# A fourth step in the stick-breaking pipeline, and four moves around it, in a two-layer decoder kernel

## The chip, the cores and the metric

The kernel is one program on one core of a Trainium2 chip. The metric is the device time of one execution in microseconds (us); the time of the kernel before is the median of three executions. One further execution was recorded by the hardware profiler, and every duration below is from that one.

## The reference

One inference step of a decoder with two layers, for a prompt of 1024 tokens and for 8 samples of one token each, which share all weights. The width is 1024, every attention has 4 heads of 128, the feed-forward width is 2816, and the memory has 256 tokens. Cut to what the change touches:

```python
# layer 0 (mixer A): gated linear recurrence beside attention into the memory
o, S = hgrn2_scan(q, k, v, logf, s0)            # a 128x128 state per head; s0 given for the samples
o = rmsnorm(o, hg_gain) * silu(g_h)             # the "gate"
om = mem_attend(q_m, mem_k, mem_v)              # softmax over 256 memory tokens
out = concatenate([o, om]) @ w_o
# layer 1 (mixer B): stick-breaking attention beside attention into the memory
z = einsum('bqhd,bkhd->bhqk', q, kf) * scale + bf
log_keep = where(mask, log_sigmoid(-z), 0.0)
tail = cumsum(log_keep, reverse) - log_keep     # for each query, over its keys
w = where(mask, exp(log_sigmoid(z) + tail), 0.0); o = einsum('bhqk,bkhd->bqhd', w, vf)
# both layers
h = h + rmsnorm(mix, g[1])
h = h + rmsnorm(swiglu(rmsnorm(h, g[2]), w_gu, w_down), g[3])
```

Outputs are the two streams, the recurrence states, the shared keys and values, and the memory's keys and values. All is in 32-bit floats.

## The kernel before

**Tiles.** The 1024 prompt tokens are two groups, 0 and 1, of G = 512; the 8 samples ride with group 1, which so has 520 columns. Activations lie with features on the 128 partitions and tokens along the row. TensorE works in a reduced-precision float, so each operand is split in a high part (a copy on ScalarE) and a low part (a subtraction on VectorE), and a product is three matmuls: high by high, high by low, low by high. Weights are split as they arrive (`split_w`, L207: a load, the copy of L217, the subtraction of L218). `proj` (L223) is such a product over 8 blocks; its matmuls are those of L231. The feed-forward block of some parts uses a seven-product scheme instead (`gate_up_w`, L619).

**Order.** The program is written as generators that yield after each step. `weave` (L187) takes streams with a declared number of steps and always advances the one whose share done, steps taken by declared steps, is least; a stream that has more steps than declared takes the rest when the others have ended. Each engine has one queue, and its order is fixed before the run by a planner: of the instructions that by its own reckoning of durations are ready, an engine gets the one that comes first in the woven program. So an instruction whose inputs are late in the plan is passed by later ones, but on the chip a queue keeps the order it was given. `tc.issue_after(x)` ties an instruction behind x on x's engine.

**Buffers.** `C()` is a pool of 4 tiles of 128x1024, `B()` of 7 tiles of 128x512, `A()` of 8 tiles of 128x1040, and `S()` of 3 banks of PSUM.

**Stick-breaking (`sb_prompt`, L1583).** Per head there are 3 units of work in group 0 and 7 in group 1. A unit is: scores on TensorE (L1594), offset and mask on VectorE (L1605 to L1609), two activations on ScalarE (`softplus`, L1580 and L1581), a running sum (L1614) and a subtraction (L1616) on VectorE, an exponential on ScalarE (L1617). The weights so made are transposed on TensorE one unit later (`turn`, L1623) and multiplied with the values two units later (`values`, L1634); `step` (L1645) holds this order. The intermediate `e` is a `B()`.

**Memory attention (`mem_attn`, L1008)** has the same shape: scores (L1032), softmax, `turn` (L1019), values (L1051), and `put` writes a head's result to the operand `xo`. For layer 0 and group 1 it runs after the gates' `merge`, beside the samples' own memory attention (`ms`) and the rest of the feed-forward block of group 0 (L1843).

**The samples' recurrence (`hgrn_sample`, L1298)** runs a head at a time: two loads of 128x1024 (the states, and the values broadcast to all partitions), three products and one sum on VectorE (L1332, L1335, L1336, L1341), a store of the states, and sums over the partitions by matmul (`total`, L1318). At the end the result goes to DRAM and back to change its layout (L1351, L1353), is transposed (L1358) and normed (L1365). It is woven beside the gate and part 1 of the feed-forward block (L1833).

**Residual (`residual`, L419)** loads the stream kept in DRAM in four pieces, all issued ahead of its loop (L428).

**The end (`close`, L807, and `out_rows`, L885).** The last down projection is made for 264 columns (three row blocks) and then for 256 (two). For each of 8 row blocks m of features: product (L823), sum (L828), square (L830), scale (L833). After m = 7 the first half of the features is transposed to rows and copied (`turn(0)`, L897, L902); `finish` sums the squares by matmul (L912), takes the root (L920, L921), and for each block of 128 tokens transposes the second half, does two fused multiply-adds (L926, L929) and stores 128x1024 (L934).

## Time and profile before

| what | value |
|---|---|
| median of three executions | 2404.62 us (2404.5 to 2404.99) |
| the profiled execution's own time | 2406.1 us |
| its span, first to last instruction | 2404.4 us |
| TensorE busy | 2377.7 us, 99% |
| VectorE busy | 1710.3 us, 71% |
| ScalarE busy | 1322.5 us, 55% |
| moved by DMA | 357.60 MB, mean 149 GB/s |

The profiled execution took 1.7 us more than its span and 1.5 us more than the median. In the rows, PE is TensorE's matmuls and PEld its weight loads, DVE is VectorE, ACT ScalarE, POOL GpSimd and SP SyncE; SPq is SyncE issuing a DMA. A row of a timeline gives start, duration, engine, line, operation, output and inputs, shapes, the number of instructions merged, and in brackets how long the engine had been idle and what ended that.

### The profile page before, as it was taken

The page shows a single profiled execution, that of the slowest core. Times are in us where ns is not written, and L with a number is a line of the kernel's source. Part 1 is how long each engine was busy: PE and PEld are TensorE (multiplying, and loading weights), DVE is VectorE, ACT ScalarE, POOL GpSimd, SP SyncE. Part 2 cuts the span into 40 slices and gives each one's busy share as a digit, 9 for nine tenths or more (in the row PEclk, how much of TensorE's full clock was granted, in tenths as well). Part 3 has the DMA queues.
Part 4 walks back from the last instruction along what each step waited for, and adds up shares of the span by engine and source line. Part 5 has one row for each costly group of instructions (what it writes and reads, how often), then busy time and mean ns, then how long its engine had stood idle before and what let it go on. Part 6 is the DMA issues. An engine that isn't in the chain of part 4 may idle for free.

```text
span 2404.4 us, 42487 instructions
## 1 busy us (share of the span) xinstructions
PE 2377.7 (99%) x15962; PEld 2156.4 (90%) x15962; DVE 1710.3 (71%) x3195; ACT 1322.5 (55%) x2736; POOL 113.7 (5%) x187
## 2 busy tenths in 40 slices
PE   9999999999999999999999999999999999999998
PEld 7888989888889988999999989877778989999998
DVE  5867558766776676878556677777776679676866
ACT  5547544454664554667544554568457566554445
POOL 1001202100000000000001200111000000000000
PEclk9999999999999999999999999999999999999999
DMA  6454766677535447332659746545354354343342
GB/s 198 122 165 119 174 199 161 164 197 193 168 106 166 134 154 232 94 101 88 193 168 225 205 152 194 161 137 156 108 154 125 95 158 137 106 129 100 113 125 76
DMA packets 514641, 357.60 MB, mean 149 GB/s; under 512 B 20173, under 2 KB 463674, under 8 KB 514434
## 3 DMA queue, kind: packets, MB, share of 16 engines
q1 hardware_dynamic: 498562, 312.93, 43.8%
q0 software_dynamic: 15872, 41.95, 7.4%
q8 instruction: 126, 2.06, 0.4%
q14 instruction: 81, 0.66, 0.1%
HBM read 322.86 MB, written 65.49 MB: 162 GB/s over the span
## 4 chain that ended last, share of the span: by engine, by line
PE 85%; DVE 6%; ACT 4%; DMA 3%; issue 2%; SPq 0%; DVEq 0%; ACTq 0%
PE mm L231 37%; PE q L619 18%; PE q L791 11%; PE q L545 4%; PE mm L1235 2%; PE s L1414 1%; DMA b<-qd 1%; PE s L1051 1%; PE s L1032 1%; PE mm L968 1%; PE mm L995 1%; PE q L823 1%; DVE ws L218 1%; ACT c L1123 1%; DVE b L1614 1%
## 5 line engine op out<-in xcount | busy, mean ns | idle before, releaser
L231 PE MATMUL mm<-x,ws 128*128 128x512 f32 (+1 forms) x5016 | 924.4, 342 | 2.2 <-ACT a L1470 1.1
L231 PEld LDWEIGHTS mm<-x,ws 128*128 128x128 f32 x5016 | 774.8, 188 | 111.4 <-ACT a L1470 1.3
L217 ACT CAST ws<-w 128x512 fp32r<-128x512 f32 x596 | 346.6, 584 | 396.1 <-PE mm L231 228.4
L218 DVE TENSOR_TENSOR ws<-w,ws 128x512 fp32r<-128x512 f32 x596 | 381.1, 646 | 238.5 <-ACT ws L217 230.5
L791 PE MATMUL q<-m,ws 128*128 128x260 f32 (+1 forms) x2496 | 303.9, 283 | 0.1
L791 PEld LDWEIGHTS q<-m,ws 128*128 128x128 f32 x2496 | 299.9, 188 | 1.0 <-ACT m L238 0.3
L619 PE MATMUL q<-y,ws 128*128 128x260 f32 (+1 forms) x1920 | 249.3, 284 | 1.9 <-DVE t L654 1.7
L619 PEld LDWEIGHTS q<-y,ws 128*128 128x128 f32 x1920 | 237.6, 188 | 3.2 <-DVE t L654 1.9
L619 PE MATMUL q<-x,ws 128*128 128x260 f32 (+1 forms) x1668 | 219.7, 283 | 1.3 <-DVE ws L614 0.7
L619 PEld LDWEIGHTS q<-x,ws 128*128 128x128 f32 x1668 | 207.7, 188 | 2.2 <-DVE ws L614 1.1
L231 PE MATMUL mm<-m,ws 128*128 128x512 f32 x768 | 186.1, 396 | 0.0
L612 ACT CAST ws<-w 128x512 fp32r<-128x512 f32 x206 | 125.0, 619 | 96.8 <-PE q L791 30.8
L231 PEld LDWEIGHTS mm<-m,ws 128*128 128x128 f32 x768 | 142.9, 188 | 32.0
L614 DVE TENSOR_TENSOR ws<-w,ws 128x512 fp32r<-128x512 f32 x206 | 139.4, 688 | 44.9 <-ACT ws L612 41.6
L800 DVE TENSOR_TENSOR r<-r,q 128x260 f32<-128x260 f32 (+1 forms) x160 | 60.6, 420 | 46.8 <-PE q L791 46.5
L545 PE MATMUL q<-x,ws 128*128 128x260 f32 (+1 forms) x720 | 87.0, 282 | 0.0
L545 PEld LDWEIGHTS q<-x,ws 128*128 128x128 f32 x720 | 86.3, 188 | 0.2
L238 ACT CAST m<-t 128x512 fp32r<-128x512 f32 (+1 forms) x88 | 54.7, 622 | 37.5 <-DVE t L860 19.8
L612 ACT CAST ws<-b 128x512 fp32r<-128x512 f32 x82 | 50.6, 620 | 42.5 <-PE q L791 13.4
L614 DVE TENSOR_TENSOR ws<-b,ws 128x512 fp32r<-128x512 f32 x82 | 56.5, 689 | 20.6 <-ACT ws L612 19.9
L239 DVE TENSOR_TENSOR m<-t,m 128x512 fp32r<-128x512 f32 (+1 forms) x88 | 60.9, 691 | 13.5 <-ACT m L238 12.5
L290 DVE TENSOR_TENSOR st<-st,n 128x512 f32<-128x512 f32 (+1 forms) x91 | 62.3, 692 | 3.7 <-ACT n L289 2.2
(422 smaller groups left out, 3117.0 us busy)
## 6 DMA issues: line engine op xcount, KB each, us to landing
w<-in_w_gu SPq DMA_DIRECT2D x275, 256.0 KB
w<-in_w_down SPq DMA_DIRECT2D x160, 256.0 KB
wsum<-in_w_gu POOLq DMA_DIRECT2D x48, 512.0 KB, 6.1
w<-in_w_in_a SPq DMA_DIRECT2D x80, 256.0 KB
w<-in_w_o SPq DMA_DIRECT2D x64, 256.0 KB
w<-wsum SPq DMA_DIRECT2D x61, 256.0 KB
b<-in_w_gu SPq DMA_DIRECT2D x39, 256.0 KB
b<-wsum SPq DMA_DIRECT2D x39, 256.0 KB
```

What stands on the lines that cost most here:

```text
L217: nc.scalar.copy(ws[:, 0, :n, :], raw[:, :n, :])
L218: split[0] = nc.vector.tensor_sub(ws[:, 1, :n, :], raw[:, :n, :], ws[:, 0, :n, :].bitcast(F32))
L231: nc.tensor.matmul(ps[:, a, : PW[g]], wt, xt[k][:, xi, o : o + PW[g]], start=(k == 0 and wi == 0), stop=(k == nk - 1 and wi == 2),)
L238: nc.scalar.copy(dst[0], src)
L239: nc.vector.tensor_sub(dst[1], src, dst[0].bitcast(F32))
L290: nc.vector.tensor_add(acc[:, :n], acc[:, :n], t[:, :n])
L545: ins = nc.tensor.matmul(pp[a][:, :h], wt, xt[k][:, xi, a * h : (a + 1) * h], start=(k == 0 and wi == 0), stop=(k == ND - 1 and wi == 2),)
L612: nc.scalar.copy(w[:, 0, :], src)
L614: split[0] = nc.vector.tensor_sub(w[:, 1, :], src, w[:, 0, :].bitcast(F32))
L619: nc.tensor.matmul(ps[:, :h], w[:, wj, k * P : (k + 1) * P], x[:, xi, :], start=(first and k == 0 and wi == 0), stop=(k == 3 and wi == 2), ...
L791: nc.tensor.matmul(pp[a][:, :h], wt, mids[k][:, xi, a * h : (a + 1) * h], start=(k == 0 and wi == 0), stop=(k == nf - 1 and wi == 2),)
L800: nc.vector.tensor_add(d, d, pp[a][:, :h])
```

## The change

Seven edits, all in the text below:

- `sb_prompt`: `step` keeps one more unit between the scores and `turn`, so that weights are transposed two units after their scores and used three units after; three closing steps instead of two; `e` is half of a `C()` tile, two units sharing one. The streams that hold it declare one step more.
- `residual`: the first two pieces are loaded ahead of the loop, the third at k = 0, the fourth at k = 2, where the stream comes from DRAM.
- `close` and `out_rows`: the first half of the features is transposed after m = 5; the scaling of m = 7 moves from ScalarE to VectorE and into a tile of its own; the transposes of the second half go feature block by feature block over all row blocks; the closing sums and the stores go by halves of 512 features.
- `mem_attn` takes a function for its result. For layer 0, group 1, it runs beside the recurrence, the gate and part 1, and its result is parked in the recurrence's key tiles (`parked`); `unpark` splits it into `xo` where the attention stood before.
- `hgrn_sample` goes by four samples (half a head): eight rounds with one `C()` each in place of four with two.
- `mixer_b.load`: the split of what is loaded is tied behind the last weight split.
- `a1.open()` stands after the weave of the recurrence.

```diff
@@ -420,13 +420,19 @@
         ht = [xpool.tile([P, 2, w], F32, tag=f"x{g}", name=nm("ht")) for _ in range(ND // 2)]
-        for j in range(ND // 2):
+
+        def fetch(j):
             if first:
 ...
                 nc.sync.dma_start(ht[j], hs[g][:, 2 * j : 2 * j + 2, :n])
+
+        for j in range(ND // 2 if first else 2):
+            fetch(j)
         for k in range(ND):
+            if not first and k % 2 == 0 and k < 4:
+                fetch(k // 2 + 2)
             if first:
@@ -830,9 +836,13 @@
                         nc.vector.tensor_add(acc, acc, sq)
-                    nc.scalar.activation(R, R, AF.Copy, scale=gcol(l, 3, m))
-                    if m == 7:
-                        list(rows.turn(0))
+                    if m < ND - 1:
+                        nc.scalar.activation(R, R, AF.Copy, scale=gcol(l, 3, m))
+                    else:
+                        rows.last = T()[:, :h]
+                        nc.vector.tensor_scalar(rows.last, R, gcol(l, 3, m), None, op0=ALU.mult)
+                    if m == 5:
+                        rows.first()
                     if m % 2:
@@ -890,18 +900,24 @@

-        def turn(self, i):
+        def first(self):
             for c, n in self.rows:
 ...
                 for k in range(4):
-                    nc.tensor.transpose(
-                        ps[:n, k * P : (k + 1) * P], self.R[4 * i + k][:, c * P : c * P + n], ident
-                    )
-                if i == 0:
-                    self.yt[c] = xpool.tile([P, D], F32, tag="x0", name=nm("yT"))
-                    nc.scalar.copy(self.yt[c][:n, :512], ps[:n, :])
-                else:
-                    yield c, n, ps
+                    nc.tensor.transpose(ps[:n, k * P : (k + 1) * P], self.R[k][:, c * P : c * P + n], ident)
+                self.yt[c] = xpool.tile([P, D], F32, tag="x0", name=nm("yT"))
+                nc.scalar.copy(self.yt[c][:n, :512], ps[:n, :])
+
+        def second(self):
+            pts = [S() for _ in self.rows]
+            for k in range(4):
+                for (c, n), ps in zip(self.rows, pts):
+                    src = self.R[4 + k][:, c * P : c * P + n]
+                    if k == 3:
+                        o = (c - 2 * self.a) * P
+                        src = self.last[:, o : o + n]
+                    nc.tensor.transpose(ps[:n, k * P : (k + 1) * P], src, ident)
+            return pts

@@ -921,19 +937,18 @@
                     rr[c0 + c] = r[:n, c : c + 1]
-            for c, n, pt in self.turn(1):
-                yt, h, rc = self.yt[c], (ht[c] if c < CH else hsm), rr[c]
-                nc.vector.scalar_tensor_tensor(
-                    yt[:n, :512], yt[:n, :512], rc, h[:n, :512], op0=ALU.mult, op1=ALU.add
-                )
-                nc.vector.scalar_tensor_tensor(
-                    yt[:n, 512:], pt[:n, :], rc, h[:n, 512:], op0=ALU.mult, op1=ALU.add
-                )
-                if c < CH:
-                    t0 = G + c * P
-                    nc.sync.dma_start(y_prompt[0, t0 : t0 + P, :], yt)
-                else:
-                    nc.sync.dma_start(y_sample.rearrange("b o d -> (b o) d"), yt[:NB])
+            pts = self.second()
+            for i in range(2):
+                s = slice(512 * i, 512 * i + 512)
+                for (c, n), pt in zip(self.rows, pts):
+                    yt, h = self.yt[c], (ht[c] if c < CH else hsm)
+                    src = pt[:n, :] if i else yt[:n, s]
+                    nc.vector.scalar_tensor_tensor(yt[:n, s], src, rr[c], h[:n, s], op0=ALU.mult, op1=ALU.add)
+                    if c < CH:
+                        t0 = G + c * P
+                        nc.sync.dma_start(y_prompt[0, t0 : t0 + P, s], yt[:, s])
+                    else:
+                        nc.sync.dma_start(y_sample.rearrange("b o d -> (b o) d")[:, s], yt[:NB, s])
                 yield
@@ -1005,7 +1020,7 @@

-    def mem_attn(g, l, qm, xo):
+    def mem_attn(g, l, qm, out):
         mkt, mv = C(), C()
@@ -1034,7 +1049,7 @@
             if pr:
-                put(xo, H + h, slice(0, G), po)
+                out(h, po)

@@ -1299,14 +1314,16 @@

-        def fetch(h):
-            st, vb = C(), C()
-            for t, src in (
-                (st, state_hgrn[0, :, h].rearrange("b k v -> k b v")),
-                (vb, vd[:, h * P : (h + 1) * P].partition_broadcast(P)),
+        def fetch(i):
+            h, a = divmod(i, 2)
+            t = C()
+            bs = slice(4 * a, 4 * a + 4)
+            for d, src in (
+                (t[:, 0], state_hgrn[0, bs, h].rearrange("b k v -> k b v")),
+                (t[:, 1], vd[bs, h * P : (h + 1) * P].partition_broadcast(P)),
             ):
-                nc.sync.dma_start(t.rearrange("p a (b v) -> p (a b) v", v=P), src)
-            return st, vb
+                nc.sync.dma_start(d.rearrange("p (b v) -> p b v", v=P), src)
+            return t

@@ -1321,28 +1338,27 @@

-        for h in range(H):
+        for h, a in ((h, a) for h in range(H) for a in range(2)):
             def col(t):
-                return t[h // 2][:, h % 2, G : G + NB].unsqueeze(2).to_broadcast([P, NB, P])
-
-            st, vb = nxt
-            nxt = h < H - 1 and fetch(h + 1)
-            stv, vbv = (t.rearrange("p a (b v) -> p (a b) v", v=P) for t in (st, vb))
+                o = G + 4 * a
+                return t[h // 2][:, h % 2, o : o + 4].unsqueeze(2).to_broadcast([P, 4, P])
+
+            st, vb = nxt[:, 0], nxt[:, 1]
+            nxt = 2 * h + a < 2 * H - 1 and fetch(2 * h + a + 1)
+            stv, vbv = (t.rearrange("p (b v) -> p b v", v=P) for t in (st, vb))
             with tc.issue_after(split[0].ins):
                 nc.vector.tensor_mul(stv, stv, col(Ft))
-            yield
             with tc.issue_after(split[0].ins):
 ...
             nc.vector.tensor_add(st, st, vb)
-            nc.sync.dma_start(st_sample[0, :, h].rearrange("b k v -> k b v"), stv)
+            nc.sync.dma_start(st_sample[0, 4 * a : 4 * a + 4, h].rearrange("b k v -> k b v"), stv)
             total()
 ...
                 nc.vector.tensor_mul(vbv, stv, col(Qt))
-            for a in range(2):
-                qs = B(F32R), B(F32R)
-                split_to(qs, vb[:, a, :])
-                late.extend((h, a, i, p) for i, p in enumerate(qs))
+            qs = B(F32R), B(F32R)
+            split_to(qs, vb)
+            late.extend((h, a, i, p) for i, p in enumerate(qs))
             yield
@@ -1517,7 +1533,18 @@
         def mem(self):
-            yield from mem_attn(self.g, 0, self.Qm, self.xo)
+            yield from mem_attn(self.g, 0, self.Qm, lambda h, po: put(self.xo, H + h, slice(0, G), po))
+
+        def parked(self, h):
+            return self.K[h // 2][:, h % 2, :G]
+
+        def mem_parked(self):
+            yield from mem_attn(self.g, 0, self.Qm, lambda h, po: nc.scalar.copy(self.parked(h), po))
+
+        def unpark(self):
+            for h in range(H):
+                put(self.xo, H + h, slice(0, G), self.parked(h))
+                yield

@@ -1607,7 +1634,10 @@
                 nc.vector.tensor_scalar(zb[:, i:o], ps[:, i:o], bh, 44.0, op0=ALU.add, op1=ALU.min)
-            e = B()
+            if not spare:
+                c = C()
+                spare.extend((c[:, 0], c[:, 1]))
+            e = spare.pop(0)
             softplus(zb, e, o)
@@ -1640,12 +1670,12 @@

-        po, asked, turned = [None, None], None, None
+        po, asked, scored, turned, spare = [None, None], None, None, None, []

         def step(new=None):
-            nonlocal asked, turned
+            nonlocal asked, scored, turned
             old, turned = turned, asked and (*asked[0], *turn(*asked[1]))
-            asked = new
+            asked, scored = scored, new
             if old:
@@ -1657,7 +1687,7 @@
                 yield
-        for _ in range(2):
+        for _ in range(3):
             step()
@@ -1700,7 +1730,8 @@
                 x = X(self.g)
-                split_to((x[:, 0, :n], x[:, 1, :n]), t)
+                with tc.issue_after(split[0].ins):
+                    split_to((x[:, 0, :n], x[:, 1, :n]), t)
                 self.xo.append(x)
@@ -1708,7 +1739,7 @@
         def mem(self):
-            yield from mem_attn(self.g, 1, self.Qm, self.xo)
+            yield from mem_attn(self.g, 1, self.Qm, lambda h, po: put(self.xo, H + h, slice(0, G), po))

@@ -1829,8 +1860,8 @@
     weave((a1.core(), 22), (f0.part(0), 14), (islice(ms, 9), 9), (islice(w0, 16), 17))
+    weave((a1.sample(), 16), (a1.gate(), 4), (a1.mem_parked(), 11), (f0.part(1), 14), (w0, 9))
     a1.open()
-    weave((a1.sample(), 16), (a1.gate(), 4), (f0.part(1), 14), (w0, 9))

@@ -1840,7 +1871,7 @@

-    weave((chain(a1.merge(), a1.mem()), 36), (ms, 74), (rest(), 33))
+    weave((chain(a1.merge(), a1.unpark()), 20), (ms, 74), (rest(), 33))
     xk0, xb0 = [], []
@@ -1854,7 +1885,7 @@
     fw = ffn_w(1, 0, o1.x, (5, 6, 5), 0, False, beside=(0, 1), src=o1.R)
-    weave((chain(b0.sb(), b0.mem()), 25), (chain(fw.part(0), fw.part(1)), 28))
+    weave((chain(b0.sb(), b0.mem()), 26), (chain(fw.part(0), fw.part(1)), 28))
     p4 = fw.part(4)
@@ -1876,7 +1907,7 @@
     weave(
-        (chain(b1.sb(), b1.mem()), 40), (chain(b1.sb_sample(), b1.mem_sample()), 76),
+        (chain(b1.sb(), b1.mem()), 41), (chain(b1.sb_sample(), b1.mem_sample()), 76),
         (chain(f0.part(0), f0.part(1), f0.part(2), islice(p3, 8)), 48),
```

## The prediction

> **What bounds the kernel now.** I read the page first, then the waits of TensorE, then the stages that the change touches.
>
> ```profile
> PE 2377.7 (99%) x15962; PEld 2156.4 (90%) x15962; DVE 1710.3 (71%) x3195; ACT 1322.5 (55%) x2736; POOL 113.7 (5%) x187
> ```
>
> TensorE is busy for 2377.7 of 2404.4 us. The change takes no matmul away. So no more than 26.7 us of idle TensorE can be won, whatever the other engines gain; the question is whose waits these are. Its waits, with total, count and longest:
>
> ```profile
> PE s L1623 <- ACT b L1617: 6.8, 8, 1.7
> ...
> PE mm L231 <- ACT a L1470: 1.1, 1, 1.1
> ...
> PE mm L231 <- DVE ws L218: 1.0, 1, 1.0
> ...
> PE s L1019 <- DVE b L1068: 0.5, 1, 0.5
> ```
>
> The largest entry is the transposing of stick-breaking weights that ScalarE has not finished: 6.8 us in 8 waits. By stage (start and end, length, then busy time of PE, PEld, DVE, ACT, POOL, clock, DMA share, GB/s), in this order the recurrence of the samples, the memory attention after it, and the two stick-breaking stages:
>
> ```profile
> 498.00:616.00 118.00, 118.00 (x606) 98.23 (x606) 80.44 (x115) 53.52 (x97) 9.41 (x16) 1.00 0.76 205
> 616.00:702.00 86.00, 85.50 (x392) 68.62 (x391) 67.53 (x131) 63.31 (x164) 0.00 (x0) 1.00 0.44 132
> 972.00:1094.00 122.00, 120.95 (x948) 115.22 (x948) 94.89 (x193) 76.91 (x165) 0.00 (x0) 1.00 0.34 102
> 1519.00:1886.00 367.00, 361.12 (x1729) 288.16 (x1728) 264.37 (x421) 225.17 (x503) 26.72 (x24) 1.00 0.45 137
> ```
>
> The stick-breaking stages leave TensorE idle for 1.05 and 5.88 us, which is the 6.8 again. The recurrence's stage leaves it nothing idle, the memory attention's 0.5 us. So one edit of the seven aims at a real wait; the others can win little and can lose.
>
> **The change part by part.** *The fourth step.* One unit, from the waits and the order of time:
>
> ```profile
> 1772.17 1.02 PE L1594 MATMUL s<-a,a 128*128 128x512 f32 x2
> ...
> 1775.94 0.62 DVE L1605 TENSOR_SCALAR b<-s,biasp 128x384 f32<-128x384 f32 x1
> ...
> 1779.48 1.02 PE L1594 MATMUL s<-a,a 128*128 128x512 f32 x2
> ...
> 1781.56 0.63 ACT L1617 ACTIVATE b<-b 128x512 f32<-128x512 f32 x1 [1.97 <-DVE b L1616]
> ...
> 1782.24 0.66 PE L1623 MATMUL s<-ident,b 128*128 128x128 f32 x4 [1.74 <-ACT b L1617]
> ```
>
> Scores at 1772.17, finished weights at 1782.19: 10.0 us, of which 2.8 pass between the end of the scores and VectorE's coming to them, behind weight splits. The next unit's scores are at 1779.48, 7.3 us later, and TensorE's queue has the transposes right behind those; it waits 1.74 us for them, and the feed-forward block's products behind them wait too. With one more unit between, the transposes stand behind the scores after that, about 7 us further on, while the longest of the 8 waits is 1.7. I take the whole 6.8 as gone. At least nothing is won, if the late engine is only waited for elsewhere; at most 12.8, the idle time of the weight loads at the same line:
>
> ```profile
> PEld s L1623 <- ACT b L1617: 12.8, 12, 2.6
> ```
>
> What it costs: the one extra closing step holds no instruction of its own. `e` in half a `C()` leaves the samples' loads two or three of four tiles in the stage at 1519. There 32 loads share 367 us, 11.5 us each; with two tiles one may live 22.9 us. From issue to use a load takes some 5.4 us (the chain below), its scaling or multiplying and the next step perhaps 10 more, an estimate, so it stays hidden. What is late next: VectorE is busy for 264 of 367 us and ScalarE for 225, so neither becomes the bound.
>
> ```profile
> 1649.99 5.41 DMA c<-in_cache_sb_v,pidx
> ```
>
> *The closing.* Rows of the end, after the last sum L828:
>
> ```profile
> 2394.92 1.04 PE L897 MATMUL s<-ident,r 128*128 128x128 f32 x8
> ...
> 2395.12 0.42 DVE L828 TENSOR_TENSOR r<-r,q 128x256 f32<-128x256 f32 x1
> 2395.55 0.58 ACT L902 COPY yT<-s 128x512 f32<-128x512 f32 x1 [0.46 <-PE s L897]
> ...
> 2396.04 0.42 ACT L830 ACTIVATE n<-r 128x256 f32<-128x256 f32 x1
> ...
> 2397.81 0.75 DVE L926 SCALAR_TENSOR_TENSOR yT<-yT,rr,hT 128x512 f32<-128x512 f32 x1 [2.27 <-ACT rr L921]
> ...
> 2400.57 0.33 SPq L934 DMA_DIRECT2D out_y_prompt<-yT  x1
> ```
>
> From the end of L828 (2395.54) to the first multiply-add (2397.81) pass 2.27 us, in which ScalarE also does two copies (the first is shown, 0.58) and the scale. With these gone from that place the square starts at once, 0.5 us earlier (2395.54 for 2396.04), and the root, which had the second copy and the scale ahead of it, I put 0.2 earlier still: 0.7 won. But the first eight transposes, 1.04 us, ran beside that wait; after m = 5 they stand on TensorE's path and push L828 back by about 0.9. The sum is +0.2. The multiply-adds stay four; the last store is issued at the same distance from the first of them, but carries 256 KB in place of 512. From its issue at 2400.57 to the end at 2404.4 pass 3.8 us. The half that goes would take 1.3 us at 205 GB/s, the rate of the stage at 498, and nothing if latency sets the end; I take 0.7, the middle. Together -0.5, between -1.1 and +0.2. For the 264 columns nothing changes: TensorE has the 256 columns' products behind them.
>
> *The residual's loads.* In the stage of the heads of layer 1, group 1, weights wait behind them:
>
> ```profile
> 1471.63 1.39 SPq L428 DMA_DIRECT2D ht<-hs  x3
> ...
> 1473.62 8.45 DMA w<-in_w_in_b
> ...
> 1489.35 2.67 PE L231 MATMUL mm<-x,ws 128*128 128x260 f32 x20 [1.01 <-DVE ws L218]
> ```
>
> TensorE waits twice afterwards, here and once for L1470: 2.1 us together, both in the waits above. But three of the four pieces still go in the first step (two ahead, the third at k = 0), so one of four leaves the burst; the waits stand 7 us after the weights landed (1482.07), behind VectorE's order. I take a quarter, -0.5, between -2.1 and +1: the fourth piece may now come late for L442, which VectorE's weight splits stand behind. The split tied in `load` adds no instruction; what hides it are the products of the block's last part, 0:
>
> ```profile
> 1308.73 40.09 PE q L619 x324
> ```
>
> *The memory attention moved.* It was not limiting where it stood (0.5 us idle); that wait, L1019 above, goes: -0.5. In the new place TensorE is never idle, so its products only lengthen the stage and shorten the next. Two costs come with it. The recurrence's `total` holds one of three `S()` banks throughout, so scores, transposes and results of the attention share two; a transpose may have to wait for a bank. The nearest row is the same L1019 wait with three banks, 0.5 once in eight; I take +0.5, between 0 and 4 (0.5 in all eight). Parking adds four copies on ScalarE of some 0.6 us, `unpark` four splits that `put` did before; ScalarE is busy for 53.5 of 118 us there, so 0. The gate's tiles come free later, as the keys stay; they now follow the memory queries, which end in that stage: 0.
>
> POOL, 9.4 us busy in that stage, makes weight sums on marks of products that don't move, and SyncE only gets the two loads of keys and values in the stage before: 0.
>
> *The recurrence by halves.* One of its four lines, its loads, and copy and subtraction of 128x512:
>
> ```profile
> L1332 DVE TENSOR_TENSOR c<-c,a x4: 1219/1219/1221, 503.7 to 559.4; 128x1024 f32<-128x1024 f32 x4
> L1308 SPq DMA_DIRECT2D c<-in_state_hgrn x4: 368/368/822, 448.9 to 536.5; - x4
> L612 ACT CAST ws<-w 128x512 fp32r<-128x512 f32 x206 | 125.0, 619 | 96.8 <-PE q L791 30.8
> ...
> L614 DVE TENSOR_TENSOR ws<-w,ws 128x512 fp32r<-128x512 f32 x206 | 139.4, 688 | 44.9 <-ACT ws L612 41.6
> ```
>
> VectorE's 16 instructions of 128x1024 at 1.22 become 32 of 128x512 at 0.69: 19.5 to 22.1 us, +2.6 of an engine with 37.6 to spare: 0. The SP queue gets 12 DMAs more (8 loads, 4 stores) at 0.37 each, 4.4 us in 118. The first load leads its use by 55 us and the last by 23; half a head ahead in place of a whole one leaves some 11, an estimate, still above a leg of 3.3 (below): 0. The place that matters is the end: the generator has 20 steps now (1 + 16 + 3), but its stream still declares 16. So the last four steps are taken when the gate, part 1 and the attention have ended:
>
> ```profile
> 598.08 1.08 PE L1318 MATMUL s<-b,selr 128*8 128x512 f32 x4
> ...
> 599.55 0.67 DVE L1349 COPY b<-s 8x512 f32<-8x512 f32 x1
> 600.25 0.30 SPq L1351 DMA_DIRECT2D od<-b  x1
> ...
> 603.57 0.31 SPq L1353 DMA_DIRECT2D b<-od  x1
> ...
> 613.00 0.41 PE L1358 MATMUL s<-ident,b 8*128 8x8 f32 x4
> ...
> 616.19 0.64 DVE L1365 SCALAR_TENSOR_TENSOR a<-ss,par,ss 128x8 f32<-128x8 f32 x4
> ```
>
> Before, TensorE had part 1 between 603 and 613. Now the chain is: last product, copy and subtraction 0.69 + 0.62 + 0.69, two matmuls 0.5, copy 0.67, two legs through DRAM at 3.3 each (600.25 to 603.57 is one), transposes to L1365 3.8: 13.6 us. Its cover is part 2 of the feed-forward block, which needs none of it and of which TensorE has eight products like this one, from the chain; the planner may bring them forward, since it passes what isn't ready:
>
> ```profile
> 652.12 5.55 PE mm L231 x24
> ```
>
> Uncovered it costs 13.6; covered, only what the plan errs on a leg by. I take +1.5, half a leg, between 0 and 13.6.
>
> Sum: -6.8 - 0.5 - 0.5 - 0.5 + 0.5 + 1.5 = -6.3 us. The profiled execution took 2406.1, 1.5 above the median of 2404.62; on the median the forecast is 2398.3.
>
> **The rivals.** *The waits move on.* Removed waits of 0.2 to 1.7 us come back where TensorE next needs VectorE: in the same stage its weights are split by an engine that is 72% busy in a fixed order. For it: the 2.8 us between scores and L1605 is VectorE's lateness, which the step doesn't cure. Against it: in that stage no wait on L218 is among TensorE's largest, and five tiles of split weights lie between. If half of the 6.8 comes back, 2401.7; if all, 2405.1: no change.
>
> *The bare end of the recurrence* (the other side). If the plan puts L1358 ahead of part 2's products, because it reckons the legs short, TensorE stands still for them. It decides when more than 12.6 of the 13.6 us are bare: 2398.3 - 1.5 + 13.6 = 2410.4, and an idle TensorE may start slowly. At the start of the kernel, after such an idle time, the first 12 products took 3.78 us and later ones 2.75:
>
> ```profile
> 7.67 3.78 PE mm L1235 x12
> ...
> 11.89 2.75 PE mm L1235 x12
> ```
>
> That adds 1.0: 2411.4. Against it: no wait of TensorE on a DMA appears past the start of the kernel in the waits. [...]
>
> *The small transfers.* [...] As a mechanism here: the stage at 498 already moves 205 GB/s at a DMA share of 0.76, and it gets 12 DMAs more, with only half a head loaded ahead. If each made VectorE's queue, and through it the weight splits, late by the 1.0 us that a late broadcast row cost it (below), 12 us come on: 2410.3. Against it: the lead of some 11 us, and that TensorE has no idle time there.
>
> ```profile
> 607.91 1.23 DVE L1098 TENSOR_TENSOR c<-c,b 128x1024 f32<-128x1024 f32 x1 [1.01 <-DMA b<-qd]
> ```
>
> **How the numbers follow.** 0.2%, 4.8 us, is about what a measurement of this kernel can tell from no change: faster is below 2399.8, slower above 2409.4. The forecast has 0.57; its own range, with the small terms at their ends, is 2392 to 2401, so a little of it counts as no change, as does nearly all of the first rival, 0.26. The bare end has 0.10, the small transfers 0.05, and 0.02 is left for orders of the plan that I don't foresee. Faster 0.58 (with the first rival's lucky part), same 0.27, slower 0.15. The range leaves out the worst of the slower cases and the best of the upper bounds: 2391 to 2409.
>
> **What would show it.** The fourth step: no L1623 among TensorE's waits, and the stage at 1519 shorter by some 6 us at the same work. The closing: L897 in two groups, one ahead of the products of m = 6; the first multiply-add about 1.7 us after the last L828; the last store's issue to the end about 3.1 us. The residual: L428 in groups of three and one. The recurrence's end: L1358 surrounded by products of part 2 and without a wait of over 2 us; a wait there of 5 us or more makes the prediction wrong, as does a stage of stick-breaking in which L231 waits for L218 as long as L1623 did.

## The result, and the profile after

The changed kernel takes 2413.88 us (median of 8 runs, 2410.02 to 2416.25), the kernel before beside it on the same chip 2405.68 us (8 runs, 2404.5 to 2408.9). The ratio is 1.0028 with a 95% interval of 1.0018 to 1.0038: slower. The profiled execution took 2412.47 us with a span of 2410.7; that of before had 2406.1 and 2404.4. So 6.3 us more of span are to be explained where I had forecast 6.3 us less. The medians differ by 8.2 us; what the single traces can't place of that is said where the terms are summed.

Line numbers below L420 are the same in both kernels; further down they have moved: the recurrence's first multiplication is L1350 now, the attention's transposes L1034, the scores L1621, `softplus` L1607 and L1608, the transposes of stick-breaking weights L1653, the group-0 feed-forward products L625. The first line of the page, of the changed kernel:

```profile
PE 2381.8 (99%) x15962; PEld 2159.9 (90%) x15962; DVE 1713.1 (71%) x3213; ACT 1324.4 (55%) x2738; POOL 112.4 (5%) x187
```

The number of matmuls is the same, 15962, but TensorE is busy for 4.1 us longer. Part of the loss is therefore no wait in the profile's sense: products that were stretched. The granted clock is at half for 3.41 us once in the middle of the changed kernel (below), and at the start its first record at full begins at 12.93 us where it did at 9.73. If half of such a time is lost, these are 1.7 and 1.6 us, estimates, 3.3 of the 4.1. TensorE's waits, of the changed kernel (total, count, longest):

```profile
PE mm L231 <- DVE ws L218: 3.3, 2, 2.4
...
PE s L1034 <- ACT b L1077: 2.8, 1, 2.8
PE q L625 <- DVE ws L620: 2.3, 4, 1.1
...
PE q L625 <- ACT ws L618: 1.5, 2, 1.3
...
PE mm L231 <- ACT b L1647: 1.2, 1, 1.2
```

The transposes of stick-breaking weights (L1623 before, 6.8 us in 8 waits) are gone from the list, as the change intends. In their place stand four others that the kernel before did not have at this size: 2.4 us once for weights of the projections (L218), 2.8 us once for the exponentials of the memory attention (L1077), and 3.8 us for split weights of the feed-forward blocks (L618 and L620), 3.0 of them beside group 0's stick-breaking. Of the last the kernel before has this much (L612 and L614 there):

```profile
PE q L619 <- DVE ws L614: 1.0, 3, 0.6
...
PE q L619 <- ACT ws L612: 0.2, 1, 0.2
```

By stage (same columns as in the prediction), of the changed kernel: recurrence with memory attention, the rest of that stage, and the two stick-breaking stages:

```profile
498.00:650.00 152.00, 148.84 (x749) 123.30 (x749) 96.07 (x172) 72.20 (x150) 8.96 (x16) 0.99 0.63 173
650.00:712.00 62.00, 61.01 (x270) 47.39 (x269) 54.49 (x91) 47.59 (x119) 0.00 (x0) 1.00 0.51 157
980.00:1107.00 127.00, 122.37 (x953) 116.08 (x952) 95.86 (x196) 78.61 (x167) 0.00 (x0) 1.00 0.38 115
1527.00:1893.00 366.00, 364.83 (x1770) 293.63 (x1768) 265.53 (x424) 227.72 (x505) 30.33 (x28) 1.00 0.47 143
```

TensorE's idle time fell from 5.88 to 1.17 us in the stage of group 1, the last row; it rose from 1.05 to 4.63 us in the stage of group 0, the third, and from 0.5 to 4.15 us in the first two, where the clock column shows 0.99 in place of 1.00.

To compare stretches of equal work I cut the trace of each kernel by TensorE's own work: each matmul counts with the median distance from its start to the next start, by its shape and line in the kernel before, and the cuts lie where the same sum is reached. This is worked out from the starts of all 15962 matmuls; in the kernel before the cuts fall at 512.2, 724.5, 985.5, 1197.1, 1503.4 and 1935.2 us. The times between them, in us:

| kernel | start | recurrence, memory attention | to group 0 | stick-breaking, group 0 | to group 1 | stick-breaking, group 1 | to the end | span |
|---|---|---|---|---|---|---|---|---|
| before | 512.2 | 212.4 | 261.0 | 211.6 | 306.3 | 431.8 | 469.2 | 2404.4 |
| after | 514.3 | 218.6 | 260.8 | 216.3 | 305.8 | 426.1 | 468.8 | 2410.7 |
| difference | +2.1 | +6.2 | -0.2 | +4.7 | -0.5 | -5.7 | -0.4 | +6.3 |

The start holds none of the edits but the move's first loads and lies between 512.2 and 514.5 in all profiled kernels of this study, so 2 us of a single execution hang on it. Between the two kernels of the table TensorE's waits for the first rows (L399) differ by 0.7 us (1.9 and 2.6), and the later rise of the clock accounts for 1.6, the estimate above. So the change does win 5.7 us where it was meant to, and loses 6.2 and 4.7 in two other places. Those two places are what the experiments had to explain.

### The profile page after: what moved, and what is told of

It is laid out like the page before. It is cut to its first block, busy times and chain, and to the rows that moved or that the text cites. A ratio compares the mean times of both kernels' runs of the same rounds, so it can differ in the third digit from the quotient of the medians.

```text
span 2410.7 us, 42477 instructions
## 1 busy us (share of the span) xinstructions
PE 2381.8 (99%) x15962; PEld 2159.9 (90%) x15962; DVE 1713.1 (71%) x3213; ACT 1324.4 (55%) x2738; POOL 112.4 (5%) x187
## 4 chain that ended last, share of the span: by engine, by line
PE 91%; DVE 4%; ACT 2%; DMA 1%; issue 1%; SPq 0%; ACTq 0%; DVEq 0%
PE mm L231 41%; PE q L625 18%; PE q L797 12%; PE q L551 4%; PE mm L1250 2%; PE s L1430 1%; PE s L1664 1%; PE s L1047 1%; PE s L1066 1%; PE s L1621 1%; PE mm L983 1%; PE mm L1010 1%; PE q L829 1%; PE s L551 1%; PE s L1034 1%
## 5 line engine op out<-in xcount | busy, mean ns | idle before, releaser
L231 PE MATMUL mm<-x,ws 128*128 128x512 f32 (+1 forms) x5016 | 929.6, 342 | 5.7 <-DVE ws L218 3.3
L231 PEld LDWEIGHTS mm<-x,ws 128*128 128x128 f32 x5016 | 776.5, 189 | 117.1 <-DVE ws L218 4.3
L218 DVE TENSOR_TENSOR ws<-w,ws 128x512 fp32r<-128x512 f32 x596 | 380.5, 645 | 222.5 <-ACT ws L217 217.9
L625 PE MATMUL q<-y,ws 128*128 128x260 f32 (+1 forms) x1920 | 250.4, 284 | 0.6 <-ACT q L633 0.4
L625 PEld LDWEIGHTS q<-y,ws 128*128 128x128 f32 x1920 | 238.0, 188 | 2.9 <-DVE ws L620 0.8
L625 PE MATMUL q<-x,ws 128*128 128x260 f32 (+1 forms) x1668 | 220.0, 283 | 3.9 <-DVE ws L620 2.1
L625 PEld LDWEIGHTS q<-x,ws 128*128 128x128 f32 x1668 | 207.8, 188 | 4.9 <-DVE ws L620 2.7
L231 PE MATMUL mm<-m,ws 128*128 128x512 f32 x768 | 186.7, 397 | 0.0
L618 ACT CAST ws<-w 128x512 fp32r<-128x512 f32 x206 | 124.9, 619 | 97.2 <-PE q L797 30.7
L231 PEld LDWEIGHTS mm<-m,ws 128*128 128x128 f32 x768 | 142.5, 188 | 32.1 <-DVE ws L218 0.2
L620 DVE TENSOR_TENSOR ws<-w,ws 128x512 fp32r<-128x512 f32 x206 | 139.3, 688 | 43.4 <-ACT ws L618 40.3
L618 ACT CAST ws<-b 128x512 fp32r<-128x512 f32 x82 | 50.6, 620 | 42.7 <-PE q L797 13.4
L239 DVE TENSOR_TENSOR m<-t,m 128x512 fp32r<-128x512 f32 (+1 forms) x88 | 60.9, 691 | 15.4 <-ACT m L238 14.5
L620 DVE TENSOR_TENSOR ws<-b,ws 128x512 fp32r<-128x512 f32 x82 | 56.4, 688 | 21.4 <-ACT ws L618 21.1
```

The source lines that it names most:

```text
L218: split[0] = nc.vector.tensor_sub(ws[:, 1, :n, :], raw[:, :n, :], ws[:, 0, :n, :].bitcast(F32))
L231: nc.tensor.matmul(ps[:, a, : PW[g]], wt, xt[k][:, xi, o : o + PW[g]], start=(k == 0 and wi == 0), stop=(k == nk - 1 and wi == 2),)
L239: nc.vector.tensor_sub(dst[1], src, dst[0].bitcast(F32))
L618: nc.scalar.copy(w[:, 0, :], src)
L620: split[0] = nc.vector.tensor_sub(w[:, 1, :], src, w[:, 0, :].bitcast(F32))
L625: nc.tensor.matmul(ps[:, :h], w[:, wj, k * P : (k + 1) * P], x[:, xi, :], start=(first and k == 0 and wi == 0), stop=(k == 3 and wi == 2), ...
```

## What stood in the two places

The chain in the recurrence's stage, of the changed kernel, in order of time:

```profile
561.22 0.69 DVE L239 TENSOR_TENSOR b<-c,b 128x512 fp32r<-128x512 f32 x1 [0.18 <-ACT b L238]
561.93 0.37 SPq L1325 DMA_DIRECT2D c<-in_state_hgrn  x1
...
567.49 0.69 DVE L1350 TENSOR_TENSOR c<-c,a 128x512 f32<-128x512 f32 x1 [3.82 <-DMA c<-in_state_hgrn]
...
569.29 0.68 DVE L1071 TENSOR_REDUCE nmx<-s 128x2 f32<-128x512 f32 x1
...
570.67 0.46 ACT L1077 ACTIVATE b<-s,nmx 128x256 f32<-128x256 f32 x1
...
571.73 0.66 PE L1034 MATMUL s<-ident,b 128*128 128x128 f32 x4 [2.80 <-ACT b L1077]
```

The load of the fifth half head (L1325) is issued at 561.93, right when the last reader of the third (L239) lets go of its tile at 561.91: the attention holds two of the four `C()` tiles for its keys and values, so the halves take turns in the other two. VectorE comes to the multiplication L1350 at 567.49 less 3.82, that is at 563.67: 1.7 us after the load was issued, while the load takes 5.6. VectorE stands still for 3.82 us, and behind L1350 in its queue stands the maximum for the memory attention (L1071), behind that ScalarE's exponentials, and behind these TensorE. Then, of the same kernel, the stretch of the wait and the one behind it:

```profile
569.00:571.70 2.70, 0.00 (x0) 0.00 (x0) 2.70 (x5) 2.64 (x8) 0.00 (x0) 1.00 0.07 22
571.70:575.00 3.30, 3.27 (x19) 3.27 (x20) 1.61 (x6) 2.17 (x4) 0.00 (x0) 0.65 0.30 86
```

After 2.8 us of idle TensorE the granted clock falls: 0.65 in the mean of 3.3 us. In the trace it is 0.5 from 572.71 on, for 3.41 us. If half of that time is lost again, it is 1.7 us, an estimate, and the profile calls TensorE busy meanwhile (3.38 us of the 3.38 from 572.72 to 576.10).

The stage of group 0, of the changed kernel:

```profile
1021.02 1.02 PE L1621 MATMUL s<-a,a 128*128 128x512 f32 x2
...
1022.32 1.03 PE L1621 MATMUL s<-a,a 128*128 128x128 f32 x4
...
1024.57 0.63 ACT L1608 ACTIVATE c<-c 128x512 f32<-128x512 f32 x1
1024.62 0.60 PE L1621 MATMUL s<-a,a 128*128 128x256 f32 x2
...
1025.75 0.63 ACT L1608 ACTIVATE c<-c 128x512 f32<-128x512 f32 x1
1026.29 0.60 ACT L618 CAST ws<-c 128x512 fp32r<-128x512 f32 x1
...
1026.94 0.51 PE L625 MATMUL q<-x,ws 128*128 128x260 f32 x2 [1.28 <-ACT ws L618]
...
1028.55 1.47 PE L625 MATMUL q<-x,ws 128*128 128x260 f32 x10 [1.10 <-DVE ws L620]
```

Scores are issued three times within 3.6 us, ScalarE does their softplus together, and the split of the weight that TensorE needs next (L618) comes behind. That weight (`c<-in_w_gu`) is late too: its load is issued at 1022.46 and has landed, by its semaphore, at 1026.23, 0.06 us before the split. Whether this order came from the fourth step or from `e` in half a `C()` tile the two traces can't say; both were changed at once.

## The experiments

Theory A: the three groups of the change act separately, and the loss is in the move with the halves and in group 0's fourth step. Rival B: `e` in `C()` tiles costs in both groups, or the small edits (loads, closing, split) shift the plan. The first runs separate the groups.

**The fourth step alone**, both groups, with `e` in `C()`; the rest as before.

```diff
-            e = B()
+            if not spare:
+                c = C()
+                spare.extend((c[:, 0], c[:, 1]))
+            e = spare.pop(0)
...
-            asked = new
+            asked, scored = scored, new
...
-        for _ in range(2):
+        for _ in range(3):
```

> The kernel before with the fourth step alone (and e in half a C tile), in both groups. Theory A: the step wins some 5.7 us in the stage of group 1 and loses some 4.8 in that of group 0, where TensorE waits for weight splits instead, so the whole stands 1 us below the kernel before. Rival: the loss in group 0 comes from the other edits' changed order and not from the step; then the whole is 6 us below.

2406.2 us (2404.26 to 2407.7) beside 2404.68 for the kernel before, ratio 1.0006 [0.9997, 1.0016]. Group 1's stretch takes 426.9 us (431.8 before), group 0's 216.8 (211.6). So the fourth step alone wins 4.9 us and loses 5.2, near the 5.7 and 4.8 of theory A: it is worth nothing as a whole that can be measured, and the two halves of it have opposite signs.

**The move of the memory attention and the halves alone.**

```diff
-    weave((a1.sample(), 16), (a1.gate(), 4), (f0.part(1), 14), (w0, 9))
+    weave((a1.sample(), 16), (a1.gate(), 4), (a1.mem_parked(), 11), (f0.part(1), 14), (w0, 9))
+    a1.open()
...
-    weave((chain(a1.merge(), a1.mem()), 36), (ms, 74), (rest(), 33))
+    weave((chain(a1.merge(), a1.unpark()), 20), (ms, 74), (rest(), 33))
```

> The kernel before with the memory attention moved beside the recurrence and the recurrence by halves, nothing else. Theory A: this pair is the largest loss, 6 to 7 us above the kernel before, with a wait of about 2.8 us of the memory attention's transposes (for the exponential, which stands behind a product of the recurrence whose states land late) and about 2 us of later waits for weight splits. Rival: these waits are an accident of the whole change's order; then it stands within 2 us of the kernel before.

2411.8 us (2409.87 to 2414.47), ratio 1.003 [1.0017, 1.0042]. The recurrence's stretch takes 218.7 us, as after the whole change (218.6). TensorE's and VectorE's waits of this kernel, one row each:

```profile
PE s L1019 <- ACT b L1062: 2.8, 1, 2.8
```

```profile
DVE c L1335 <- DMA c<-in_state_hgrn: 3.8, 1, 3.8
```

They are the same two waits as after the whole change (there L1034 and L1350), with the same half clock behind them (at 571.8; the mean clock of this execution is 0.997, and 0.999 in the kernel before). This group carries most of the slowdown: 7.1 us by the medians, where theory A had 6 to 7.

**The rest alone**: residual loads, closing by halves, the tied split.

```diff
-        for j in range(ND // 2):
+        for j in range(ND // 2 if first else 2):
...
-                    if m == 7:
-                        list(rows.turn(0))
+                    if m == 5:
+                        rows.first()
...
-                split_to((x[:, 0, :n], x[:, 1, :n]), t)
+                with tc.issue_after(split[0].ins):
+                    split_to((x[:, 0, :n], x[:, 1, :n]), t)
```

> The kernel before with the spread residual loads, the closing by halves and the tied split of the load alone. Theory A: next to nothing, 0 to 2 us below the kernel before (0.2 at the end, and up to 2 us that may go at the last products of the block of layer 1, group 0). Rival: the spread loads cost the 1.4 us that the heads of layer 1, group 1, wait longer in the changed kernel; then it stands 1 to 2 us above.

2406.22 us, ratio 1.0005 [0.9996, 1.0015]: no change that can be measured. No stretch moves by more than 0.8 us, but for the start (513.5) and the one up to group 1 (304.1 for 306.3), where the kernel before has a wait of 1.7 us at 1349 that comes and goes between kernels with the same code there: with the fourth step in group 1 only, the stretch takes 304.0, in the next run, which differs only behind it, 306.1. The total lies where the rival put it, but the longer wait of the rival isn't there: that for L218 is 0.8 us (1.0 before). The medians of these three runs lie 1.5, 7.1 and 1.5 us above the kernel before; their sum, 10.2, agrees with the 8.2 of the whole change within the intervals, as it should if the groups act separately.

**The fourth step in group 1 only.** Group 0 keeps three steps, two closing ones, and `e` in `B()`.

```diff
-            if not spare:
+            if g and not spare:
...
-            e = spare.pop(0)
+            e = spare.pop(0) if g else B()
...
-            asked, scored = scored, new
+            asked, scored = (scored, new) if g else (new, None)
```

> The kernel before with the fourth step in group 1 alone; group 0 keeps three steps and e in a B tile. Theory A: the gain of group 1 without the loss of group 0, 5 to 6 us below the kernel before. Rival: the gain in group 1 needs nothing from group 0 but is noise of the order; then it stands within 2 us of the kernel before, and no nearer to it than the first kernel of this set.

2401.52 us (2400.3 to 2402.89), ratio 0.9987 [0.9977, 0.9997]: faster than both kernels, though by 3.2 us where theory A had 5 to 6. Group 0's stretch is back at 211.1 us, group 1's at 428.4. One wait of group 1 is new and large in this kernel:

```profile
PE mm L231 <- ACT b L1620: 1.9, 1, 1.9
```

It ends at 1741.9, VectorE having waited 3.3 us for a samples' load of keys (`in_cache_mem_k`) at 1730.9, and the clock falls to half at 1742.6 (0.998 in the mean of the execution). That raised the question whether `e` in `C()` makes the samples' loads late here, and whether group 1 would do better without it.

**The same with `e` in `B()`.**

```diff
-            if g and not spare:
-                c = C()
-                spare.extend((c[:, 0], c[:, 1]))
-            e = spare.pop(0) if g else B()
+            e = B()
```

> As the last kernel of the first set (fourth step in group 1 alone), but e stays in a B tile. Theory B: half a C tile for e takes from the samples' loads and makes the 1.9 us wait at 1742 with the 3.4 us of half clock behind it; without it the stage of group 1 is some 3.5 us shorter, 6 to 7 us below the kernel before. Rival: the B tiles, of which the samples' broadcast rows need one each, are then short instead, and it stands no better, 2 to 4 us below, with waits on the broadcast rows.

2404.29 us beside 2406.97 before, ratio 0.9988 [0.9978, 0.9997]. The group-1 stretch takes 428.7 us where it took 428.4. The wait of 1.9 us and the fall of the clock are gone (0.999 in the mean), but a wait of 1.8 us on the issue of instructions (at 1680) stands in their place. So in group 1 the place of `e` makes no difference that can be measured; my theory that it costs there was not borne out. What single traces can tell here is limited: by cuts of the same kind, the stretch of group 1 takes 429.7 to 434.9 us in the nine profiled kernels in which group 1 is as before, and 426.1 to 428.9 in the five with the fourth step there. The ranges don't overlap and the means differ by 4.2 us; the 5.7 of the whole change is the upper end.

For group 0 the two halves of the edit were then taken one at a time.

**Group 0, four steps, `e` in `B()`** (group 1 as before).

```diff
-            asked = new
+            asked, scored = (scored, new) if not g else (new, None)
...
-        for _ in range(2):
+        for _ in range(3 if not g else 2):
```

> The kernel before with the fourth step in group 0 alone, e in B tiles. Theory C1: the deeper pipeline holds the values of a head one unit longer, the next head's keys and values load late, units bunch, and TensorE loses some 4.8 us at 1020 to 1060 as in the whole change. Theory C2: the loss comes from e in C tiles; then this stage loses at most what it lost before.

2406.09 us in one timing, beside 2406.97. Group 0's stretch takes 212.0 us (211.6 before). The stage of this kernel, same columns:

```profile
972.00:1100.00 128.00, 127.06 (x991) 121.02 (x991) 100.35 (x204) 82.12 (x174) 0.00 (x0) 1.00 0.35 104
```

0.94 us idle in 128. The fourth step by itself costs nothing in group 0, and wins nothing.

**Group 0, three steps, `e` in `C()`** (group 1 as before).

```diff
-            e = B()
+            if not g and not spare:
+                c = C()
+                spare.extend((c[:, 0], c[:, 1]))
+            e = B() if g else spare.pop(0)
```

> The kernel before with e in half a C tile in group 0 alone, three steps kept. Theory C1 (depth): the stage of group 0 stands as before, within 1 us. Theory C2 (C tiles): it loses some 4.8 us more at 1020 to 1060.

2411.77 us in one timing, beside 2406.97. Group 0's stretch takes 216.8 us: the whole loss is there without the fourth step. Of this kernel, the wait, then the stage and the stretch behind the wait:

```profile
1019.08 0.51 PE L619 MATMUL q<-x,ws 128*128 128x260 f32 x2 [2.48 <-ACT ws L612]
```

```profile
972.00:1100.00 128.00, 123.96 (x961) 118.09 (x960) 95.83 (x195) 78.77 (x168) 0.00 (x0) 0.99 0.38 114
1019.00:1023.00 4.00, 3.44 (x15) 2.84 (x15) 3.32 (x7) 1.88 (x4) 0.00 (x0) 0.61 0.21 56
```

4.04 us idle, 2.48 of them in one wait for a weight split, and the clock at 0.61 behind it. So in group 0 it is the tiles. `ffn_w`, which runs beside it, keeps two of the four `C()` tiles for its weights (`c<-in_w_gu`, L579 here). Their first load before, from the issues of SyncE, and then the first four of them in this kernel:

```profile
940.25 0.42 SPq L579 DMA_DIRECT2D c<-in_w_gu  x1
```

```profile
1014.59 2.08 SPq L579 DMA_DIRECT2D c<-in_w_gu  x4
```

The weight that was loaded some 60 us ahead of its split (1001.15) before is now loaded 3.8 us ahead of it: by its semaphore it has landed at 1018.18, the split L612 starts at 1018.42, and TensorE waits for that split until 1019.08. In all three profiled kernels with group 0's `e` in `C()` these loads begin at 1014.6 to 1022.5; in the other eleven, the one with four steps in `B()` among them, at 940.3 to 948.5. So the price is a lost lead here too. Why the planner puts the loads that late, with `e` in the same pool, I did not isolate.

That left the recurrence. Theory L: the halves' loads are late because only one `C()` tile is left to load ahead. Rival S: the generator has 20 steps and declares 16, so its end is left to the end of the stage. The runs by halves without the move, with and without the right number, and the move with each suspect taken out, tell them apart.

**The halves alone**, the attention where it was.

```diff
-        def fetch(h):
-            st, vb = C(), C()
+        def fetch(i):
+            h, a = divmod(i, 2)
+            t = C()
...
-        for h in range(H):
+        for h, a in ((h, a) for h in range(H) for a in range(2)):
```

> The kernel before with the recurrence by halves alone; the memory attention stays where it was, so all four C tiles are the recurrence's. Theory A: the late load of a half comes from the two tiles that the moved attention holds, so VectorE has no wait of over 1 us for the states here, TensorE none of over 1 us in the stage, and the whole is within 1 us of the kernel before. Rival: half a head is too short a lead in any case; then the wait of some 3.8 us on VectorE is there too, though the transposes that made TensorE wait for it are not, and the end of the recurrence, with 20 steps under a declared 16, shows at the seam of the stages.

2412.71 us in one timing, beside 2406.97, the recurrence's stretch 219.1 us: the whole loss again, but by another way. No load of the states is late, as theory A had it, but its total fails; of the rival only the late end of the recurrence came. Of this kernel, VectorE's and TensorE's rows in the stretch where the time goes, and the stage from 600 to 705:

```profile
635.15 1.21 DVE L1101 TENSOR_REDUCE sc<-c 128x8 f32<-128x1024 f32 x1
...
636.88 1.22 DVE L1098 TENSOR_TENSOR c<-c,b 128x1024 f32<-128x1024 f32 x1
...
639.23 0.69 DVE L218 TENSOR_TENSOR ws<-w,ws 128x512 fp32r<-128x512 f32 x1
...
639.97 2.36 PE L231 MATMUL mm<-x,ws 128*128 128x512 f32 x9 [1.58 <-DVE ws L218]
```

```profile
600.00:705.00 105.00, 100.16 (x449) 79.28 (x448) 79.15 (x145) 66.36 (x174) 0.00 (x0) 0.99 0.53 158
```

The weight split L218 stands behind the samples' 1.2 us multiplications and sums (L1098, L1101), because the end of the recurrence, the merge and the samples' memory attention have fallen onto the same stretch. 4.84 us of 105 are idle. The last of these waits, 1.84 us, ends at 701.9, and behind it the clock falls to half at 702.2:

```profile
701.90:707.00 5.10, 5.06 (x17) 4.19 (x18) 3.54 (x9) 1.31 (x3) 0.00 (x0) 0.67 0.17 51
```

**The halves alone, 20 steps declared.**

```diff
-    weave((a1.sample(), 16), (a1.gate(), 4), (f0.part(1), 14), (w0, 9))
+    weave((a1.sample(), 20), (a1.gate(), 4), (f0.part(1), 14), (w0, 9))
```

> The recurrence by halves alone, as in the run before of that name, but its stream declares 20 steps and not 16, so that all its steps, the end of the recurrence among them, are spread evenly over the stage. Theory S (the halves lose their 6.8 us because the last four steps are left to the end of the stage): the subtraction of the results and the merge start some 5 us or more earlier than with 16 declared, TensorE's lost time from 560 to 700 us of its work falls back to within 2 us of the kernel before, no wait of TensorE above 1.5 us is left there, total 2403 to 2407. Rival T (what costs is the bunching of the shorter VectorE instructions with the samples' multiplications, whatever the number declared): at least 4 of the 6.8 us stay lost in the same stretch, total 2409 or more.

2403.68 us in one timing; the kernel before took 2405.18 in the median (15 runs, 2402.69 to 2407.07). The recurrence's stretch takes 213.1 us instead of 219.1. One number in the plan is worth 6.0 us, of which the fall of the clock at 702.2, gone here, is 1.7, an estimate. The first multiplication of the eight halves in the kernel with 16 declared, and then in that with 20 (first and last start):

```profile
L1335 DVE TENSOR_TENSOR c<-c,a x8: 683/686/689, 505.2 to 606.8; 128x512 f32<-128x512 f32 x8
```

```profile
L1335 DVE TENSOR_TENSOR c<-c,a x8: 683/684/687, 505.1 to 577.4; 128x512 f32<-128x512 f32 x8
```

With 16 declared the last half begins 29.4 us later, and everything behind it too. The same stage with 20 declared:

```profile
600.00:705.00 105.00, 103.96 (x476) 83.32 (x475) 80.98 (x152) 69.90 (x180) 0.00 (x0) 1.00 0.51 149
```

1.04 us idle instead of 4.84. Without the move, theory S holds and the halves cost nearly nothing.

**The move with 20 steps declared.**

```diff
-    weave((a1.sample(), 16), (a1.gate(), 4), (a1.mem_parked(), 11), (f0.part(1), 14), (w0, 9))
+    weave((a1.sample(), 20), (a1.gate(), 4), (a1.mem_parked(), 11), (f0.part(1), 14), (w0, 9))
```

> The move of the memory attention and the halves, without the fourth step and the rest, with 20 steps declared for the recurrence in place of 16. Theory L (here the loss comes from the half-head loads, which can only be issued when the half before is done, and not from the steps declared): VectorE still waits 2 us or more for a load of the states, TensorE for the softmax of the attention behind it, the loss from 495 to 700 us of work stays within 2 us of that with 16 declared, total 2409 to 2414. Rival S (the declared number is the cause here too): the wait of 2.8 us and the half clock behind it go, total 2403 to 2407.

2410.7 us in one timing, beside 2405.18; the recurrence's stretch 216.9 us (218.7 with 16, 212.4 before). Only 1.8 us come back. VectorE's wait in the stage, of this kernel:

```profile
DVE c L1335 <- DMA c<-in_state_hgrn: 6.8, 4, 2.5
```

With the steps spread evenly the lateness is spread too: four waits with 6.8 us in all, where it was one of 3.8. TensorE's wait behind them is 1.5 in place of 2.8, and the clock stays up (1.0 in the mean of the execution). Of the 1.8 us that come back, 1.7 is the half clock that stayed out, an estimate. So with the move the declared number only distributes the lateness. Whether the loads are its cause is for the next run.

**The move without the later loads**: those of the last four half heads are left out and a constant fills their tiles, so this kernel's results are other numbers.

```diff
+            if i > 3:
+                nc.gpsimd.memset(t, 0.5)
+                return t
```

> The move of the memory attention and the halves, with the loads of the states and values of the last four half heads left out (their tiles are filled with a constant by POOL, so the states and results of those half heads are other numbers). Theory L (late loads): VectorE's wait of 3.8 us for the state's load goes, with it the 2.8 us that TensorE waits for the attention's exponentials and the half clock behind them; 4 to 5 us of the 9.2 us lost between 495 and 560 us of work come back, total 2406 to 2409. Rival (the two banks of scores, or VectorE's order, make TensorE wait there and the load only happens to end last): the wait for the exponentials stays at 2 us or more and the total stays at 2411 to 2414.

2409.37 us in one timing, beside 2405.18; the recurrence's stretch 214.0 us, 4.7 less than with the loads. TensorE's rows of this kernel where the wait was:

```profile
566.45 1.18 PE L231 MATMUL mm<-x,ws 128*128 128x260 f32 x7
567.60 0.66 PE L1019 MATMUL s<-ident,b 128*128 128x128 f32 x4
568.01 7.26 PE L231 MATMUL mm<-x,ws 128*128 128x260 f32 x50
```

The transposes follow without a wait, and the clock doesn't fall there (0.999 in the mean of the execution, as in the kernel before). Of the 6.3 us that the move and the halves cost in this stretch, 4.7 hang on the late loads. The 1.6 that are left I did not separate: the steps declared, the two banks and the four copies are candidates. The wait of 2.8 us and the half clock, 1.7 by estimate, make 4.5 of the 4.7. The price rests on this stretch and not on the totals: the spans of the two profiled executions, 2412.8 with the loads and 2407.6 without, differ by 5.2, but the first was the longest of six and has two more falls of the clock, at 1670.8 and 1790.3 (0.997 in the mean, 0.999 without the loads); against the median with the loads, 2411.8, the single timing is 2.4 us lower, 0.4 above the range that theory L gave. The edit also takes 2.1 MB of loads out of the stage, so that a lighter DMA load is part of what was tested. The move with whole heads was not run; what it would cost without the halves stays open.

**The fourth step in group 1 together with the rest**, the attention and the recurrence as before.

```diff
-            if not spare:
+            if g and not spare:
...
-            asked, scored = scored, new
+            asked, scored = (scored, new) if g else (new, None)
...
-        for j in range(ND // 2):
+        for j in range(ND // 2 if first else 2):
...
-                    if m == 7:
-                        list(rows.turn(0))
+                    if m == 5:
+                        rows.first()
```

> The fourth step in group 1 alone (group 0 as before) together with the spread residual loads, the closing by halves and the tied split; the memory attention and the recurrence as before. If the parts add, the gain of the fourth step in group 1 alone (ratio 0.9987 with 0.9977 to 0.9997) stays and the rest adds nothing that can be measured: 2400 to 2403 where the kernel before takes 2404.6, ratio 0.998 to 0.9995. If the order that the planner finds changes with the small parts so much that each sum of parts is a draw of its own: anything from 2398 to 2408.

2402.36 us (11 runs, 2398.74 to 2404.18) beside 2405.18 (15 runs), ratio 0.9987 [0.9978, 0.9996]: the same as without the rest. The recurrence and group 0 take 212.4 and 211.0 us, group 1 428.9. This is one of three versions of the change that beat both kernels, by some 3 us; the other two are group 1 alone with `e` in `C()` and in `B()`.

## Why the prediction was wrong

*The fourth step, -6.8.* Right for the place it was read from, wrong for the other. In group 1 the L1623 waits went, the idle time fell by 4.7 us and the stretch by 5.7; alone, by 4.9, and in the three other runs that have it, by 2.9 to 3.4. I had forecast 5.9 there. The rival that the waits move on got a part of it: L231 waits for the exponential 1.2 us after the change, 2.2 with the fourth step alone, and 1.9, with a fall of the clock behind it (at 1742.6), and 2.4 in the two runs with the step in group 1 only and `e` in `C()`. In group 0 I booked the 1.05 us of idle time as won and priced the new tiles nowhere. The sentence "so it stays hidden" was worked out for the samples' loads of group 1, which share four `C()` tiles with `e`; that group 0 has another user of these tiles, the weights of `ffn_w`, did not enter the sum. There it cost 4.7 us, shown by the tiles alone (216.8 us) and the step alone (212.0): the weights' loads lost their lead of some 60 us.

*The recurrence by halves, loads: 0.* This is the step that failed with the largest price. I took the lead of a half-head load as "some 11 us, an estimate, still above a leg of 3.3". Both numbers were off. The lead was worked out from an even spacing of the halves, and each edit was priced by itself: that the moved attention holds two of the four `C()` tiles did not enter it. In the trace a half's load waits for the tile of the half two before it, and VectorE came to use it 1.7 us behind its issue; in the halves alone, with four tiles, no load was late. And the leg was the wrong row: 3.3 us is a transfer of a small row through DRAM; this load took 5.6 us from issue to use. The price is 4.7 us (the stretch with and without the loads). The last of my rivals came nearest, with a VectorE made late by half-head loads and its queue behind it, and I gave it 0.05 because I set that same lead against it. But it put the lateness down to 12 more transfers in a busy stage, with 1.0 us each; the runs show one load that could not be issued earlier, 3.8 us, with a half clock behind it.

*The recurrence by halves, end: +1.5, or 13.6 bare.* The bare end did not come. The row of the changed kernel:

```profile
638.40 0.30 SPq L1367 DMA_DIRECT2D od<-b  x1
...
641.77 0.30 SPq L1369 DMA_DIRECT2D b<-od  x1
...
644.02 0.41 PE L1374 MATMUL s<-ident,b 8*128 8x8 f32 x4
```

Products of part 2 fill the time of both legs, as forecast, with no wait of TensorE on a DMA. The 20 steps under 16 declared cost 1.8 us with the move (218.7 against 216.9), near the 1.5. But without the move the same mismatch costs 6.0, and not through bare legs: the end falls onto other streams' VectorE work. The term had the right size here by luck: 1.7 of the 1.8 is a fall of the clock, an estimate, which the sum did not have.

*The memory attention moved, -0.5 + 0.5.* Its wait at L1019 of before went, and a wait of 2.8 us came at the same instruction (L1034 now) in the new place, not for a bank but for VectorE behind the late load. I had costed the move as if VectorE's queue had slack of its own ("37.6 to spare"); slack in the mean of the stage does not help an instruction that stands behind a wait.

*The closing, -0.5.* The parts about as forecast, the sum not. Of the changed kernel: last sum, first multiply-add, stores.

```profile
2402.43 0.42 DVE L834 TENSOR_TENSOR r<-r,q 128x256 f32<-128x256 f32 x1
...
2404.72 1.42 DVE L946 SCALAR_TENSOR_TENSOR yT<-yT,rr,hT 128x512 f32<-128x512 f32 x2 [1.48 <-ACT rr L937]
2405.50 2.32 SPq L949 DMA_DIRECT2D out_y_prompt<-yT  x4
```

From the end of the last sum (2402.85) to the first multiply-add pass 1.87 us (before 2.27; forecast 1.7), from the last sum to the end of the span 7.85 (before 8.86). That is 1.0 us won behind the last sum. The transposes that now stand ahead of the products take 1.04 us on TensorE's path, a little more than the 0.9 I had reckoned, so nothing of note is left, and the run with the rest alone shows no gain.

*The residual's loads, -0.5.* The loads go as the edit says, but the issue doesn't look like "three and one", and the wait behind it grew. Of the changed kernel, SP's queue and TensorE:

```profile
1481.95 0.47 SPq L429 DMA_DIRECT2D ht<-hs  x1
...
1483.86 1.39 SPq L429 DMA_DIRECT2D ht<-hs  x3
```

```profile
1501.74 1.47 PE L231 MATMUL mm<-x,ws 128*128 128x260 f32 x10 [2.42 <-DVE ws L218]
```

That is 2.42 us where 1.01 stood, 1.4 more, and beyond the +1 that I had set as this term's bound. In the runs with this edit but without the others in the stage (the rest alone, and with group 1's step) the wait stays at 0.8, so this edit alone doesn't make it; which of the others does, together with it or without, I did not separate.

*The clock.* The sum has no term for a fall of the clock in the kernel's middle. In the changed kernel the clock was at 0.5 for 3.41 us from 572.71, behind the wait of 2.80 us; the section at the end has the other waits. By estimate (half of 3.41) this is 1.7 us of the 6.2 in the recurrence's stretch.

The sum with the measured terms, by stretches: -5.7 (group 1), +4.7 (group 0), +6.2 (recurrence and attention), about -1 for the rest, and +2.1 at the start, which isn't the change's. So the traces place 4.2 us of the change's own loss. The medians differ by 8.2, with an interval of 4.3 to 9.1 (the ratio's, on 2405.68); where the rest lies, one trace of each kernel can't show.

## What to carry over

A tile pool is a resource like an engine: before an edit takes a tile from a pool or halves a prefetch, list every stream that draws on that pool in every stage where the edit runs, and price the load from the instant its tile comes free to the instant its user's turn comes, not from the mean spacing. Most of both losses of this change hung on loads that had lost their lead in the same pool. A wait that one engine's queue takes on is paid by everything behind it (here 3.82 us on VectorE became 2.80 on TensorE), so look for whose instructions stand there. And when a generator gets more steps, the number that the planner is told must be changed with it: here 16 for 20 cost 6.0 us in the halves alone, with the same work to do.
